# Gate and up of both SwiGLUs by Strassen's scheme for 18 of 22 column tiles, in a one-core fp32r layer kernel

## The chip, the cores and the metric

The kernel runs on one core of one Trainium2 chip. The metric is the device time of one execution in microseconds. The kernel before took 1068.85 us (median of three runs, 1068.67 to 1070.68). A core has TensorE (PE: matmuls, and the weight loads PEld), VectorE (DVE), ScalarE (ACT), GpSimd (POOL) and SyncE (SP). Each of them takes its own list of instructions in order; a semaphore lets an instruction wait for one of another engine.

## The reference

One layer on x of 512 rows by 1024 columns, in float32: a SwiGLU, a token mixer and a second SwiGLU, each between norms, with shift, scale and gate from a conditioning vector c.

```
mod = silu(c) @ w_ada + b_ada                    # 9 x 1024: shift, scale, gate of 3 sub-layers
h = modulate(x, norm_pre_g, shift, scale)        # rms norm, * (1 + scale) + shift
h = swiglu(h, w_gate, w_up, w_down)              # (silu(h @ w_gate) * (h @ w_up)) @ w_down
x = x + 0.5 * (1 + gate) * rms_norm(h, norm_post_g)
x = x + (1 + gate) * rms_norm(hybrid_mixer(...)) # spatial gating and forgetting attention
x = x + 0.5 * (1 + gate) * rms_norm(swiglu(...)) # the second SwiGLU, with its own weights
```

w_gate and w_up are 1024 by 2816 for each SwiGLU, w_down is 2816 by 1024. 2816 columns are 22 column tiles of 128; 1024 rows are 8 blocks (k) of 128.

## The kernel before, in words

x lies transposed, as 8 blocks of 128 features by 512 tokens; "half" below is 256 tokens. Every matmul multiplies fp32r operands that are split into a high part and a low part, and `mm3` makes three matmuls of one product: high by high, high by low, low by high (weights are the stationary side). So a weight comes by DMA on SP's queue as float32 (`raw`, two buffers of 1 MB, `load_next`), ScalarE copies it to its rounded high part (`Pair.hi`, line 192), and VectorE subtracts that from the raw weight for the low part (`Pair.lo`, line 196). `load_next` for the next buffer is issued when both low parts of one are done.

A SwiGLU (`ffn`) goes through its 22 column tiles in three groups of 7, 7 and 8 (`GROUPS`). For a column tile, `gate_up` makes 24 matmuls of 128x512 for gate (PSUM tile `pg`) and 24 for up (`pu`). `activate` then reads them: silu on ScalarE (line 452), times up on VectorE (453), copy to the high part on ScalarE (454), subtraction for the low part on VectorE (457); the tile `h` that results is an operand of down. When a group's tiles are through, down goes over 8 output tiles (`pd`, three matmuls per column tile of the group), which are copied to `y` by ScalarE for the first group (520) and added to it by VectorE for the others (522). The last group's down goes by halves, with the sums of squares for the norm that follows. `ahead` prepares the weights of a later unit after each tile. `between` loads a 512 KB slice of w_ada (`mraw`) and reduces it on VectorE (275); it lies in the first SwiGLU and in the beginning of the mixer only.

The order of the instructions on every engine is the order in which the program is written (`manual_schedule`). In the first SwiGLU the string `START` sets the first three column tiles, beside the norm of x. The second SwiGLU begins beside the mixer's last norm, with four tiles by halves. PSUM has six buffers of 512 columns for all of this (`ps_mm`), and the split weights have eight buffers (`wp`).

## Time and profile before

| | before |
|---|---|
| median of three runs | 1068.85 us |
| the profiled execution, its own time | 1069.54 us |
| its span | 1067.8 us |
| mean granted TensorE clock | 0.965 |
| matmuls | 5246, busy 1012.6 us (95%) |
| VectorE | 983 instructions, busy 567.0 us (53%) |
| ScalarE | 655 instructions, busy 376.4 us (35%) |
| GpSimd | 114 instructions, busy 142.0 us (13%) |
| moved by DMA | 128.82 MB, mean 121 GB/s |

The span is the time from the first to the last instruction of the profiled execution; 1.7 us of its time lie around the span. Busy shares are means over stages with different limits, so a stage is read by its own windows. The first SwiGLU lies from about 60 us to 330 us, the second from about 670 us to the end. A matmul's bar is longer than its step: matmuls are pipelined, so the step from one start to the next is what it costs.

### The profile page before, as it was taken

How to read it: one execution, taken by the hardware profiler on the slowest of the kernel's cores; microseconds unless marked ns; L12 is line 12 of the kernel's file. 1: busy time of each engine (PE TensorE's matmuls, PEld its weight loads, DVE VectorE, ACT ScalarE, POOL GpSimd, SP SyncE). 2: the span in 40 equal slices, each digit the busy share in tenths (PEclk: the TensorE clock that was granted, in tenths of full speed). 3: DMA queues.
4: the chain of work that ended last, by engine and by line, in shares of the span. 5: the costliest groups of instructions: out<-in, count | busy, mean ns of one | idle time of the engine just before them, and what ended most of it. 6: DMA issues, size and time to landing. Idle time of an engine off the chain costs nothing.

```text
span 1067.8 us, 13094 instructions
## 1 busy us (share of the span) xinstructions
PE 1012.6 (95%) x5246; PEld 852.4 (80%) x5246; DVE 567.0 (53%) x983; ACT 376.4 (35%) x655; POOL 142.0 (13%) x114
## 2 busy tenths in 40 slices
PE   6999999999999998899999997799999999999995
PEld 5778888888888997787778687798888888888894
DVE  3876454646443469757756668855222324333434
ACT  5243232322232333444546453534233222222331
POOL 0000000000000036216115135500000000000023
PEclk8899999999999998999999788989999999999998
DMA  8735555456444313241112112114232223232101
GB/s 331 286 139 204 208 202 208 173 179 223 160 142 153 137 62 122 99 147 66 64 35 95 40 41 79 40 41 148 109 119 79 94 84 118 79 109 89 40 21 60
DMA packets 27037, 128.82 MB, mean 121 GB/s; under 512 B 3040, under 2 KB 5472, under 8 KB 18656
## 3 DMA queue, kind: packets, MB, share of 16 engines
q1 hardware_dynamic: 26976, 127.99, 33.6%
q8 instruction: 41, 0.67, 0.2%
q14 instruction: 20, 0.16, 0.0%
HBM read 125.88 MB, written 2.10 MB: 120 GB/s over the span
## 4 chain that ended last, share of the span: by engine, by line
PE 77%; DVE 14%; ACT 3%; DMA 2%; issue 2%; POOL 2%; SPq 0%; DVEq 0%; POOLq 0%; ACTq 0%
PE pu L211 7%; PE pg L209 7%; PE pu L210 7%; PE pg L211 7%; PE pg L210 7%; PE pu L209 7%; PE pd L211 6%; PE pd L209 6%; PE pd L210 6%; DVE mraw L275 2%; DMA mraw<-w_ada 1%; DVE z L362 1%; DVE xm L393 1%; PE pqk L209 1%; PE ps_s L924 1%
## 5 line engine op out<-in xcount | busy, mean ns | idle before, releaser
L192 ACT CAST wu<-raw 128x1024 fp32r<-128x1024 f32 (+2 forms) x164 | 162.3, 1025 | 57.5 <-PE pd L211 53.3
L196 DVE TENSOR_TENSOR wu<-raw,wu 128x1024 fp32r<-128x1024 f32 (+1 forms) x130 | 151.5, 1205 | 58.6 <-ACT wu L192 58.0
L211 PE MATMUL pd<-h,wu 128*128 128x256 f32 (+1 forms) x480 | 160.2, 334 | 0.0
L209 PE MATMUL pd<-h,wu 128*128 128x256 f32 (+1 forms) x480 | 160.1, 333 | 0.0
L210 PE MATMUL pd<-h,wu 128*128 128x256 f32 (+1 forms) x480 | 159.7, 333 | 0.0
L453 DVE TENSOR_TENSOR sg<-sg,pu 128x512 f32<-128x512 f32 (+1 forms) x48 | 30.8, 642 | 230.9 <-PE pu L211 224.2
L250 POOL TENSOR_TENSOR ssum<-ssum,sq 128x256 f32<-128x256 f32 x59 | 47.3, 803 | 776.1 <-ACT sq L249 774.7
L209 PE MATMUL pg<-xm,wu 128*128 128x512 f32 (+1 forms) x360 | 136.1, 378 | 0.0
L211 PE MATMUL pu<-xm,wu 128*128 128x512 f32 (+1 forms) x360 | 136.0, 378 | 0.0
L211 PE MATMUL pg<-xm,wu 128*128 128x512 f32 (+1 forms) x360 | 135.5, 376 | 0.0
L210 PE MATMUL pg<-xm,wu 128*128 128x512 f32 (+1 forms) x360 | 135.1, 375 | 0.0
L210 PE MATMUL pu<-xm,wu 128*128 128x512 f32 (+1 forms) x360 | 134.7, 374 | 0.0
L209 PE MATMUL pu<-xm,wu 128*128 128x512 f32 (+1 forms) x360 | 134.5, 374 | 0.0
L454 ACT CAST h<-sg 128x512 fp32r<-128x512 f32 (+1 forms) x48 | 28.2, 587 | 224.6 <-DVE sg L453 224.6
L210 PEld LDWEIGHTS pd<-h,wu 128*128 128x128 f32 x480 | 90.3, 188 | 10.3
L211 PEld LDWEIGHTS pd<-h,wu 128*128 128x128 f32 x480 | 90.5, 189 | 9.8
L209 PEld LDWEIGHTS pd<-h,wu 128*128 128x128 f32 x480 | 90.1, 188 | 9.7
L196 POOL TENSOR_TENSOR wu<-raw,wu 128x1024 fp32r<-128x1024 f32 (+1 forms) x28 | 69.4, 2488 | 77.3 <-ACT wu L192 77.3
L210 PEld LDWEIGHTS pu<-xm,wu 128*128 128x128 f32 x360 | 68.5, 190 | 13.8
L210 PEld LDWEIGHTS pg<-xm,wu 128*128 128x128 f32 x360 | 68.7, 191 | 13.3
L211 PEld LDWEIGHTS pg<-xm,wu 128*128 128x128 f32 x360 | 68.4, 190 | 13.2
L209 PEld LDWEIGHTS pg<-xm,wu 128*128 128x128 f32 x360 | 68.6, 190 | 12.9
(229 smaller groups left out, 1616.1 us busy)
## 6 DMA issues: line engine op xcount, KB each, us to landing
raw<-wgu SPq DMA_DIRECT2D x43, 1024.0 KB, 4.8
mraw<-w_ada SPq DMA_DIRECT2D x49, 512.0 KB, 3.9
raw<-wd SPq DMA_DIRECT2D x16, 896.0 KB, 4.5
mrawh<-w_ada SPq DMA_DIRECT2D x19, 512.0 KB, 5.1
raw<-wd SPq DMA_DIRECT2D x8, 1024.0 KB, 4.8
raw<-wz SPq DMA_DIRECT2D x4, 1024.0 KB, 4.7
raw<-wqk SPq DMA_DIRECT2D x4, 1024.0 KB, 5.4
raw<-wo SPq DMA_DIRECT2D x4, 1024.0 KB, 4.9
```

Of the source, the lines that this page charges most:

```text
L192: nc.scalar.copy(self.u[j][:, 0, : self.n], self.raw[:, j * self.n : (j + 1) * self.n])
L196: (eng or nc.vector).tensor_sub(u[:, 1, :n], self.raw[:, j * n : (j + 1) * n], u[:, 0, :n].bitcast(F32))
L209: nc.tensor.matmul(ps, lhsT=lh, rhs=rh, start=start, stop=False)
L210: nc.tensor.matmul(ps, lhsT=lh, rhs=rl, start=False, stop=False)
L211: nc.tensor.matmul(ps, lhsT=ll, rhs=rh, start=False, stop=stop)
L250: eng.tensor_add(self.acc, self.acc, sq)
L275: nc.vector.scalar_tensor_tensor(raw, raw, 1.0, crow, op0=ALU.mult, op1=ALU.mult, accum_out=msum[:, j * KT + kt : j * KT + kt + 1])
L362: nc.vector.scalar_tensor_tensor(z[k], ysl(k, cs), G2[i][:, k : k + 1], r, op0=ALU.mult, op1=ALU.mult)
L393: nc.vector.scalar_tensor_tensor(xm[k - 2][:, 1, cs], t[k - 2], shift(i, k - 2), xm[k - 2][:, 0, cs].bitcast(F32), op0=ALU.add, op1=ALU.su ...
L453: nc.vector.tensor_mul(sg, sg, pu[:, :n])
L454: nc.scalar.copy(h[f][:, 0, cs], sg)
L924: nc.tensor.matmul(ps[:, :n], lhsT=sel[:, h : h + 1].broadcast_to([P, P]), rhs=cum[:, :n], start=False, stop=False)
```

## The change

`GROUPS` becomes 4, 4, 4, 4 and 6 column tiles. The four tiles of group 0 are made as before. The other 18 are made in nine pairs. For a pair, the two column tiles, the two halves of the tokens and the two halves of the 1024 features (four blocks k each) make 2x2 blocks: a11, a12, a21, a22 of x (first index: half of the tokens, second: half of the features), and b(kh, fh) of the weights (half of the features, tile). Instead of eight products of blocks there are seven, of sums of blocks. Gate and up lie side by side in one PSUM bank, so a `product` is 2 (gate, up) x 4 blocks k x 3 = 24 matmuls of 256 columns. The order is 1, 2 of the first pair, then per pair 6, 5, 7, 1 of the next pair, 3, 2 of the next pair, 4.

`sums_of_x` makes the four sums S1 to S4 of x's blocks once in each SwiGLU, each in high and low part, in the course of group 0. `prepare` makes the weights of a pair: W1, W2, W3 are split from the raw weights; T5 = b01 - b00 and T7 = b11 - b01 are made by a negating copy on ScalarE (line 687) and a DMA of GpSimd's queue that adds the other block onto it in SBUF (688); T6 and T4 are differences on VectorE (694); all four are then split (702, 703). `evictions` adds up the products: ScalarE copies bank a three times (m1, u2, u3, line 623), VectorE adds bank b or c to the copies (636), and silu, multiplication, copy and subtraction follow for each quarter (637, 613, 615, 616). The list `blocks` holds the matmuls, and `at(b, ...)` puts a piece of work of the other engines ahead of block b. The w_ada slices become halves of 256 KB, of which `between` reduces one after nearly every product of the first SwiGLU. `hp` has 4 buffers of twice the size.

```diff
-GROUPS = (range(0, 7), range(7, 14), range(14, 22))
+GROUPS = (range(0, 4), range(4, 8), range(8, 12), range(12, 16), range(16, 22))
+    def sums_of_x():
+        S = {n: htile([P, KT // 2, 2, HT], F32R, f"S{n}") for n in (1, 2, 3, 4)}
...
+            def split(n, v):
+                hi, lo = (S[n][:, 2 * q : 2 * q + 2, part] for part in range(2))
+                nc.scalar.copy(hi, v)
+                sub(lo, v, hi.bitcast(F32))
...
+            for n, op, b, c in ((1, add, a21, a22), (3, sub, a11, a21)):
+                v[n], low = temp(), temp()
+                op(v[n], b[0], c[0])
+                op(low, b[1], c[1])
+                yield 1.2
+                add(v[n], v[n], low)
+                split(n, v[n])
...
+        def product(p, n):
+            b, fresh = {1: ("a", True), 2: ("b", True), 5: ("c", True), 6: ("a", False), 7: ("a", False), 3: ("c", False), 4: ("a", False)}[n]
+            def work():
+                if fresh:
+                    bank[p, b] = ps_mm.tile([P, 2, HT], F32, tag="mm", name=f"bank_{b}")
+                ps, w = bank[p, b], W[p, n]
+                for e in range(2):
+                    for k in range(KT // 2):
+                        c = slice(k * P, (k + 1) * P)
+                        t = mm3(ps[:, e], w[:, e, 0, c], w[:, e, 1, c], moving(n, k, 0), moving(n, k, 1), fresh and e + k == 0, e == 1 and k == KT // 2 - 1, not fresh)
+                    tick(4 * t)
+                if i == 0 and (n != 6 or p % 4 == 0):
+                    between()
...
+            for name, src, b, fh, cs, after in (("c11", "m1", "b", 0, T1ST, c[2]), ("c22", "u3", "c", 1, T2ND, c[7]),
+                                                ("c12", "u2", "c", 1, T1ST, c[3])):
+                first, second = both(name, src, b, fh, cs)
+                at(after + 1, first)
+                at(after + 2, second)
+            first, second = gated(p, "c21", 0, T2ND, None)
+            at(c[4] + 1, first)
+            at(c[4] + 1, second)
...
+            def added(n, then, minus, plus):
+                def work():
+                    t = sum_of(n, True, then)()
+                    nc.scalar.activation(t, b(*minus), AF.Copy, scale=-1.0)
+                    nc.gpsimd.dma_start(t, b(*plus), accum_op=ALU.add)
...
+            at(c[6] - 5, added(5, 6, (0, 0), (0, 1)))
+            at(c[1] - 2, plain(1, 0, 0))
+            at(c[6] - 4, added(7, 4, (0, 1), (1, 1)))
+            at(c[2] - 2, plain(2, 1, 0))
+            at(c[6] - 3, minus(6, 1, 5))
+            at(c[6] - 2, split(6))
+            at(c[6] - 2, minus(4, 0, 6))
+            at(c[6] - 1, plain(3, 1, 1))
+            at(c[5] - 1, split(5))
+            at(c[7] - 1, split(7))
+            at(c[4] - 5, split(4))
```

In the orders below a row has the line, the operation, the tile written and the tiles read; the numbers behind the names tell the buffers apart, and `128x2x512` is the weight of a product, gate and up side by side. First VectorE, before, in the middle of the first SwiGLU's first group: for a column tile two low parts of weights (196), then the multiplication and the low part of `h` (453, 457).

```order
L196 TENSOR_TENSOR wu_511<-raw_491,wu_511 128x1024
L196 TENSOR_TENSOR wu_514<-raw_491,wu_514 128x1024
L453 TENSOR_TENSOR sg_520<-sg_520,pu_281 128x512
L457 TENSOR_TENSOR h1_519<-sg_520,h1_519 128x512
L196 TENSOR_TENSOR wu_525<-raw_499,wu_525 128x1024
L196 TENSOR_TENSOR wu_528<-raw_499,wu_528 128x1024
L453 TENSOR_TENSOR sg_534<-sg_534,pu_359 128x512
```

Now VectorE with the change, in the second SwiGLU's group 1, from the addition for c22 of the first pair to the last of what stands ahead of W5's low part for the second pair (the weights and T tiles are of the second pair, the `q` tiles of the first but for q_7604, which is c11 of the second).

```order
L636 TENSOR_TENSOR q_7564<-q_7564,bank_c_7512 128x512
L680 TENSOR_TENSOR W2_7573<-raw_7441,W2_7573 128x2x512
L613 TENSOR_TENSOR q_7564<-q_7564 128x256
L616 TENSOR_TENSOR h2_7500<-q_7564,h2_7500 128x256
L694 TENSOR_TENSOR T5_7537<-raw_7441,T5_7537 128x1024
L636 TENSOR_TENSOR q_7497<-q_7497,bank_c_7512 128x512
L703 TENSOR_TENSOR W6_7633<-T5_7537,W6_7633 128x2x512
L694 TENSOR_TENSOR T7_7568<-raw_7441,T5_7537 128x1024
L613 TENSOR_TENSOR q_7497<-q_7497 128x256
L616 TENSOR_TENSOR h2_7500<-q_7497,h2_7500 128x256
L636 TENSOR_TENSOR q_7604<-q_7604,bank_b_7637 128x512
L680 TENSOR_TENSOR W3_7667<-raw_7441,W3_7667 128x2x512
```

Behind these come a low part of a down weight, the multiplications and low parts of c21 and c11, and then W5's low part. Additions, multiplications and low parts of the pair that ends now stand between the low parts and the differences of the pair that comes. ScalarE at the same place, from the copy m1 of the second pair to the high part of its W5:

```order
L623 COPY q_7604<-bank_a_7576 128x512
L637 ACTIVATE q_7497<-q_7497 128x256
L702 CAST W6_7633<-T5_7537 128x2x512
L615 CAST h2_7500<-q_7497 128x256
L637 ACTIVATE q_7604<-q_7604 128x256
L679 CAST W3_7667<-raw_7441 128x2x512
L194 CAST wu_7696<-raw_7571 128x512
L608 ACTIVATE q_7699<-bank_a_7411 128x256
L615 CAST h2_7500<-q_7699 128x256
L615 CAST h3_7705<-q_7604 128x256
L702 CAST W5_7708<-T5_7537 128x2x512
```

The high parts of W6, W3 and W5 now each stand behind a silu or a copy whose input VectorE has to make first.

The third place is VectorE in the first SwiGLU's group 0, with the change, where the last plain tile (sg_609) is activated.

```order
L198 TENSOR_TENSOR wu_521<-raw_492,wu_521 128x512
L444 TENSOR_TENSOR sx_542<-xm0_193,xm4_342 128x512
L445 TENSOR_TENSOR sx_543<-xm0_193,xm4_342 128x512
L447 TENSOR_TENSOR sx_542<-sx_542,sx_543 128x512
L438 TENSOR_TENSOR S1_538<-sx_542,S1_538 128x2x256
...
L438 TENSOR_TENSOR S1_538<-sx_602,S1_538 128x2x256
L507 TENSOR_TENSOR sg_609<-sg_609,pu_525 128x512
L509 TENSOR_TENSOR h1_507<-sg_609,h1_507 128x512
```

Eighteen rows of the sums of x, five of them subtractions behind a copy of ScalarE, now stand ahead of that tile's multiplication.

More of the change, by code (lines that the diff above doesn't have):

```diff
@@ new lines, in ffn, with moving @@
+        raw, W, bank = {}, {}, {}
+        def moving(n, k, part):
+            if n in (1, 2, 4):
+                return xm[k + (n != 1) * KT // 2][:, part, T2ND if n == 4 else T1ST]
+            return forms[{5: 1, 6: 2, 7: 3, 3: 4}[n]][:, k, part, :]
+        def product(p, n):
[10 more added lines that the diff above has]
+                if i == 0 and (n != 6 or p % 4 == 0):
+                    between()
+                W.pop((p, n))
+            return block(24 * HT * MM, work)
@@ new lines, in ffn, with expect_ffn @@
+        for b, (us, work) in enumerate(blocks):
+            for what in todo.pop(b, ()):
+                what()
+            if not forms and b >= KT:
+                finish_side(side_s)
+            work()
+        for b in sorted(todo):
+            for what in todo[b]:
+                what()
+        forms.clear()
+    def expect_ffn(s):
+        for g, fs in enumerate(GROUPS):
+            if g == 0:
+                for f in fs:
+                    expect(a["wgu"][s, f], 2 * D)
+            else:
+                for p in range((fs[0] - PLAIN) // 2, (fs[-1] + 1 - PLAIN) // 2):
+                    for kh in range(2):
+                        expect(a["wst"][s, p, kh], 4 * T)
+            for m in range(KT // 2):
+                expect(a[f"wd{g}"][s, m], 2 * len(fs) * P)
```

458 lines of the change are left out of this document (307 added, 151 removed).

## The prediction

> **What bounds the kernel now.** I read the chain of waits first, then the engines' busy time by stage in three FFN windows (columns: window, length, busy time of PE, PEld, VectorE, ScalarE, GpSimd, granted clock, DMA share, GB/s).
>
> ```profile
> PE 1012.6 (95%) x5246; PEld 852.4 (80%) x5246; DVE 567.0 (53%) x983; ACT 376.4 (35%) x655; POOL 142.0 (13%) x114
> PE 77%; DVE 14%; ACT 3%; DMA 2%; issue 2%; POOL 2%; SPq 0%; DVEq 0%; POOLq 0%; ACTq 0%
> 125.00:190.00 65.00, 65.00 (x283) 52.72 (x282) 34.13 (x48) 19.98 (x26) 0.00 (x0) 1.00 0.55 198
> 750.00:800.00 50.00, 50.00 (x217) 40.57 (x216) 14.03 (x14) 15.00 (x20) 0.00 (x0) 1.00 0.29 100
> 800.00:850.00 50.00, 50.00 (x217) 40.49 (x216) 15.82 (x17) 14.73 (x19) 0.00 (x0) 1.00 0.24 85
> ```
>
> In the FFNs TensorE is busy in the whole window at full clock; VectorE works 34.1 of 65 us in the first FFN (which has the w_ada reductions) and 14 to 16 of 50 in the second. So matmuls taken out count in full, as long as the other engines keep up in the order in which they are now asked to. What a matmul costs is the step between starts:
>
> ```profile
> 339.76 0.40 PE L209 MATMUL pg<-xm,wu 128*128 128x512 f32 x1
> 349.94 0.40 PE L211 MATMUL pg<-xm,wu 128*128 128x512 f32 x1
> ...
> 1014.79 0.27 PE L209 MATMUL pd<-h,wu 128*128 128x256 f32 x1
> 1016.87 0.27 PE L209 MATMUL pd<-h,wu 128*128 128x256 f32 x1
> ```
>
> The first two are 44 steps apart: 10.18 / 44 = 0.231 us for 512 columns. The others are 18 apart: 0.1156 for 256. A step is 0.45 ns per column, and 256 columns lose nothing to the weight load.
>
> **The matmuls removed.** A pair took 2 x 48 x 0.2304 = 22.12 us; seven products of 24 x 0.1152 = 2.765 take 19.35. Eighteen pairs (nine per FFN) save 18 x 2.765 = **49.8 us**. Down's columns stay: the other grouping moves no work of TensorE's. The added matmuls are all of shapes that these rows price, so this term has no range.
>
> **The steady pair.** What was 2 low parts of weights and 2 operations of an activation per tile becomes a tight weave. The prices:
>
> ```profile
> L192 ACT CAST wu<-raw 128x1024 fp32r<-128x1024 f32 x128 | 129.7, 1046 | 57.5 <-PE pd L211 53.3 <-issue 3.6 <-DMA raw<-wgu 0.4
> L520 ACT COPY y<-pd 128x512 f32<-128x512 f32 x16 | 9.4, 588 | 52.1 <-PE pd L211 52.1
> L522 DVE TENSOR_TENSOR y<-y,pd 128x512 f32<-128x512 f32 x16 | 11.0, 688 | 36.6 <-PE pd L211 36.6
> 803.91 2.36 DVE L196 TENSOR_TENSOR wu<-raw,wu 128x1024 fp32r<-128x1024 f32 x2 [7.38 <-ACT wu L192]
> 704.80 0.36 ACT L452 ACTIVATE sg<-pg 128x256 f32<-128x256 f32 x1
> 705.20 0.42 DVE L453 TENSOR_TENSOR sg<-sg,pu 128x256 f32<-128x256 f32 x1 [0.45 <-ACT sg L452]
> 705.66 0.41 ACT L454 CAST h<-sg 128x256 fp32r<-128x256 f32 x1 [0.49 <-DVE sg L453]
> 706.10 0.43 DVE L457 TENSOR_TENSOR h<-sg,h 128x256 fp32r<-128x256 f32 x1 [0.47 <-ACT h L454]
> ```
>
> A 1024-wide copy on ScalarE is 1.05 (the negating copy I price alike), a 1024-wide subtraction or difference on VectorE 2.36 / 2 = 1.18, a 512-wide copy out of PSUM 0.59, a 512-wide addition 0.69; a quarter's silu 0.36, multiplication 0.42, copy 0.41, low part 0.43, with 0.04 from one engine's end to the other's start. Now I walk down the two orders from the end of product 7 of one pair to W5's low part for the next (primes: of the next pair). Both queues are in order, and nearly each row waits for the other engine's last one.
>
> - u3 copy 0.59, c22 addition 0.69, silu 0.36, T7' negation 1.05, W2' high 1.05, low 1.18, c22 multiplication, copy, low part 1.26: 6.18.
> - T6' difference 1.18, c12 addition 0.69, silu 0.36, W6' high 1.05, low 1.18: 4.46.
> - T4' difference 1.18, c12's three 1.26, c11' addition 0.69, silu 0.36, W3' high 1.05, low 1.18: 5.72.
> - c21's three 1.26, c11' multiplication and copy 0.83, W5' high 1.05, low 1.18: 4.32.
>
> Together 20.7, and 16 hand-overs of 0.04 make it 21.3. TensorE has five products in that time (1', 3, 2', 4, 6'), and the first two matmuls of product 5', which need no low part: 5 x 2.765 + 0.23 = 14.05. So it stands still for about **7.3 us** ahead of product 5' in each pair that has a pair before it in its group. Groups of 2, 2, 2 and 3 pairs have 1 + 1 + 1 + 2 = 5 such pairs: 5 x 7.3 = 36.5 us in the second FFN. The bounds: if no row waited for the other engine, VectorE's own rows of the stretch are 5 x 1.18 (W2', T6', W6', T4', W3') + 1.18 (W5') + 3 x 0.69 + 3 x 0.85 + 0.42 = 12.1 us, which fits, and nothing is lost; if the negation and each of VectorE's 1024-wide rows took the 1.22 of the reduction below, it is 21.3 + 0.4 and a stall of 7.7. I take the walk, since an order of single handed-over rows leaves nothing to overlap.
>
> In the first FFN `between` puts one more reduction ahead of each block.
>
> ```profile
> 374.82 1.22 DVE L275 SCALAR_TENSOR_TENSOR mraw<-mraw,crow 128x1024 f32<-128x1024 f32 x1 [2.89 <-DMA mraw<-w_ada]
> ```
>
> At half the width that is 1.22 - (1.18 - 0.69) = 0.73. Five lie on the walk, 3.65 less what falls into waits: I take 3.5, so 10.8 us, times 5 = **54 us** (0 to 5 x 11.0).
>
> **First pairs and group ends.** The first pair of a group has no earlier pair's quarters between its weights, but W5 and W7 still stand behind c11's chain: product 2 to W5's low part is addition 0.69, silu 0.36, high 1.05, low 1.18 plus hops, 3.4, against product 6's 2.77 and 0.23: 0.4 to 0.6, and product 7 another 0.4. I take 0.95, with a reduction or two in the first FFN 1.45: 4 x 0.95 + 4 x 1.45 = 9.6 (0 to 16). At a group's end c21 (0.36 + 1.26 + hops, 1.8) is covered by one part of down, 12 matmuls of 0.1152 = 1.38: 0.4 in each of six, 2.4.
>
> **Group 0.** The START's last rows on VectorE, and a copy:
>
> ```profile
> 67.92 0.68 DVE L453 TENSOR_TENSOR sg<-sg,pu 128x512 f32<-128x512 f32 x1
> 68.64 0.62 ACT L454 CAST h<-sg 128x512 fp32r<-128x512 f32 x1 [1.58 <-DVE sg L453]
> 69.29 0.69 DVE L457 TENSOR_TENSOR h<-sg,h 128x512 fp32r<-128x512 f32 x1 [0.69 <-ACT h L454]
> ...
> 69.54 0.39 PE L209 MATMUL pg<-xm,wu 128*128 128x512 f32 x1
> ```
>
> TensorE begins the fourth plain tile at 69.54, is through 11.06 later at 80.6, and after the 9 matmuls of down on the first three tiles (2.07) needs the fourth at 82.7. VectorE ends the first tile at 69.98; two more activations take 2.1 each (74.2), three half-size low parts 2.1 (76.3), 18 rows of sums at 0.69 take 12.4 (88.7), five of which wait 0.7 for a copy (92.2), multiplication and copy 1.3: 93.5, which is **10.8 us** late. In the second FFN the same rows stand ahead of the last split tile's activations; I take 10.8 again, 21.6 for both (0, if the rows find slack, to 28 rows x 0.69 x 2 = 38.6).
>
> **What a standstill costs after it.** The granted clock (window, length, busy TensorE, clock, DMA share, GB/s) around three gaps that the kernel already has:
>
> ```profile
> 658.00:660.00 2.00, 0.00 (x0) 0.62 0.00 0
> 660.00:662.00 2.00, 0.58 (x3) 0.50 0.00 0
> 662.00:664.00 2.00, 2.00 (x11) 0.50 1.00 291
> 664.00:666.00 2.00, 2.00 (x13) 0.67 0.56 234
> 666.00:668.00 2.00, 2.00 (x19) 1.00 0.00 0
> ...
> 678.00:680.00 2.00, 1.07 (x3) 0.74 0.57 139
> 680.00:682.00 2.00, 2.00 (x11) 0.50 0.92 385
> ...
> 696.00:698.00 2.00, 1.85 (x8) 0.51 0.58 106
> 698.00:700.00 2.00, 2.00 (x12) 0.50 0.98 414
> 700.00:702.00 2.00, 2.00 (x11) 0.50 0.04 12
> 702.00:704.00 2.00, 2.00 (x16) 0.78 0.00 0
> ```
>
> The busy time lost (busy x (1 - clock)) is 0.29 + 1.0 + 0.66 = 1.95, 0.28 + 1.0 = 1.28 and 0.91 + 1.0 + 1.0 + 0.44 = 3.35: mean 2.2. Twelve long gaps (10 pairs, 2 groups 0) cost 12 x 2.2 = **26.4 us** (0 if a gap of 7 us in a period of 26 is too short to be punished, 40 at 3.35). [...]
>
> **The added DMAs.** T5 has some 7 us from the end of its negation to T6's difference, which needs it. No accumulating DMA is in the trace; loads are:
>
> ```profile
> raw<-wgu SPq DMA_DIRECT2D x43, 1024.0 KB, 4.8
> raw<-wsT SPq DMA_DIRECT2D x1, 512.0 KB, 3.2
> raw<-wqk SPq DMA_DIRECT2D x4, 1024.0 KB, 5.4
> ```
>
> It reads two 512 KB operands and writes one: between the 3.2 of 512 KB and, at three times 512 KB, 3.2 + 2 x 1.6 = 6.4. Either is hidden, so I take 0. At 10 us T6 and all that stands behind it would come 3 us later in each pair: 18 x 3 = 54 us. [...]
>
> **Sum**: -49.8 + 36.5 + 54 + 9.6 + 2.4 + 21.6 + 26.4 = +100.7. Against the profiled execution's 1069.5 that is 1170.2; the median lies 0.7 below, so **1169.5 us**.
>
> **Rivals.** *The queues keep up.* VectorE's and ScalarE's busy time fits the pair (12.1 us of 14), and if most hand-overs overlapped, what is left is group 0 and the group ends: -49.8 + 9.6 + 2.4, or 1031 us. For it speaks that VectorE works 14 to 16 us of 50 now; against it that a queue in order stands still while it waits, and the walk has one open row at a time. 12%. *Lighter stalls.* The walk is right in kind, but a third of its waits falls into others: two thirds of the 124 us of the stalls above (36.5 + 54 + 9.6 + 2.4 + 21.6) are 83, and the clock costs 12 x 1.28 to 12 x 2.2: -49.8 + 83 + 15 to 26 is +48 to +59 on 1068.85, 1117 to 1128, with some play 1105 to 1140. For it speaks that in the trace a second copy of ScalarE regularly runs beside VectorE's first row; against it that here the rows belong to one another. 18%. *The accumulating DMA is late*, being the place where T6 waits: from 7 us on it decides; at 10 us half of the 54 us comes on top of stalls that partly take it in, 1200 to 1225. For it speaks that nothing of its kind is in the trace, against it the 6.4 us above. 13%. *The change leaves the time as it was*, savings and stalls cancelling out: 3%; nothing picks that point.
>
> **How the numbers follow.** Forecast 54%, 1169.5, its own range 1140 to 1200 by the bounds of clock and group 0. 1105 to 1212 holds the lighter stalls too and half of the late DMA: 54 + 18 + 6.5 = 78.5%. Faster by over 0.2% (2 us, what a measurement of this kernel can tell): 12%; within: 3%; slower: 85%.
>
> **What would show it.** In the changed profile, TensorE's idle time ahead of line 211 for `bank_c` (product 5) should be 7 to 11 us, 10 times, ended by VectorE's line 703 or ScalarE's 702 of W5; the idle ahead of down in group 0 about 10, ended by lines 508 and 509 of `h`; PEclk about 0.5 in the windows behind. Steps inside products stay at 0.115. Line 694 (T6) should not be ended by a DMA. I am wrong if the gaps ahead of product 5 are under 3 us, or if T6's row waits for GpSimd's queue.

## The result and the profile after

The changed kernel takes **1213.71 us** (median of four runs, 1213.61 to 1216.19), the kernel before in the same comparison 1068.76 (1068.46 to 1070.68): 1.1358 times as long, with a 95% interval of 1.1338 to 1.1377. The forecast was 1169.5 us, with a range up to 1212. The direction and the mechanism of the largest term were right. The forecast is 44 us too low, and the measured time lies 1.7 us above the range.

The page of the changed kernel (busy time by engine, the chain of waits, the two dearest groups of product 5, and the accumulating DMA with its median time to landing):

```profile
span 1211.8 us, 16389 instructions
PE 1030.9 (85%) x6398; PEld 916.5 (76%) x6398; DVE 776.7 (64%) x1438; ACT 517.1 (43%) x917; POOL 181.2 (15%) x148
PE 45%; DVE 27%; ACT 12%; DMA 9%; issue 5%; POOL 2%; SPq 0%; ACTq 0%; DVEq 0%; POOLq 0%
L211 PE MATMUL bank_c<-S,W 128*128 128x256 f32 x288 | 96.8, 336 | 81.3 <-ACT W L702 81.2
L213 PE MATMUL bank_c<-S,W 128*128 128x256 f32 x288 | 95.5, 331 | 8.7 <-DVE W L703 8.7
T<-raw POOLq DMA_DIRECT2D x36, 512.0 KB, 6.1
```

TensorE's share of the chain falls from 77% to 45%, and VectorE's, ScalarE's and the DMA's grow to 27, 12 and 9%. 81.2 of the idle microseconds stand ahead of one group of matmuls, the first of a product 5. The stages (columns as in the prediction's windows), first of the changed kernel, then of the one before. The first stage ends where the statistics of the first half of the first FFN's output begin, at 383 us in the kernel before (its gate and up go on until 358, later than the 330 us named ahead of the prediction):

```profile
69.50:473.20 403.70, 334.02 (x2113) 304.03 (x2112) 267.45 (x479) 161.65 (x253) 26.11 (x24) 0.89 0.54 162
473.20:754.40 281.20, 251.66 (x1440) 210.90 (x1439) 191.72 (x443) 134.12 (x309) 103.40 (x70) 0.92 0.20 69
754.40:1211.80 457.40, 386.66 (x2590) 354.81 (x2590) 274.56 (x442) 194.58 (x322) 51.46 (x51) 0.93 0.37 103
```

```profile
69.50:383.00 313.50, 313.02 (x1453) 258.34 (x1451) 161.21 (x229) 90.49 (x120) 4.45 (x6) 1.00 0.51 184
383.00:661.40 278.40, 255.43 (x1492) 215.10 (x1492) 199.82 (x438) 134.56 (x309) 103.25 (x70) 0.93 0.21 74
661.40:1067.80 406.40, 384.98 (x2038) 330.88 (x2038) 162.83 (x242) 124.19 (x192) 34.11 (x35) 0.97 0.24 83
```

The first FFN grows by 90.2 us, the mixer by 2.8, the second FFN by 51.0. TensorE's idle time in the first FFN goes from 0.5 us to 69.7, and VectorE works 267 us there instead of 161.

**A steady pair** in the second FFN, TensorE at the hand-over from product 6' to product 5', and the granted clock around it (engine columns as above, clock third from the end):

```profile
888.50 0.28 PE L213 MATMUL bank_a<-S,W 128*128 128x256 f32 x1
894.32 0.58 PE L211 MATMUL bank_c<-S,W 128*128 128x256 f32 x1 [5.54 <-ACT W L702]
894.70 0.42 PE L212 MATMUL bank_c<-S,W 128*128 128x256 f32 x1
895.58 0.58 PE L213 MATMUL bank_c<-S,W 128*128 128x256 f32 x1 [0.46 <-DVE W L703]
```

```profile
892.00:894.00 2.00, 0.00 (x0) 0.00 (x0) 1.19 (x3) 1.12 (x3) 0.00 (x0) 0.50 0.63 231
894.00:896.00 2.00, 1.22 (x4) 0.92 (x5) 1.50 (x2) 2.00 (x4) 0.00 (x0) 0.50 0.00 0
896.00:898.00 2.00, 2.00 (x11) 2.00 (x11) 2.00 (x2) 0.65 (x1) 0.00 (x0) 0.50 0.03 8
898.00:900.00 2.00, 2.00 (x18) 2.00 (x18) 0.78 (x2) 0.62 (x1) 0.00 (x0) 0.93 0.00 0
```

The product behind product 7 of the pair before started at 874.34, and the first matmul that needs W5's low part starts 21.2 us later; the walk in the prediction came to 21.3. The clock is at half until about 898, and product 5 of the steady pairs takes 5.2 to 5.9 us instead of 2.86, the wait for its low part included. Ahead of product 5 the ten steady pairs wait 8.35, 7.53, 7.53, 7.13, 6.94 us in the first FFN and 5.54, 5.49, 5.54, 4.83, 4.89 in the second.

**A first pair**, group 2 of the first FFN. Rows of ScalarE, GpSimd, VectorE and TensorE, put in order of time: the negation for T5, its DMA, T6 (which needs T5), the high part of W6, product 5.

```profile
189.51 1.06 ACT L687 ACTIVATE T<-raw 128x1024 f32<-128x1024 f32 x1 [5.23 <-DMA raw<-wst]
190.87 1.19 POOL L688 DMA_DIRECT2D T<-raw  x1 [50.25 <-DVE mraw L272]
198.91 1.23 DVE L694 TENSOR_TENSOR T<-raw,T 128x1024 f32<-128x1024 f32 x1 [1.41 <-DMA T<-raw]
200.25 1.05 ACT L702 CAST W<-T 128x1024 fp32r<-128x1024 f32 x1 [4.13 <-DVE T L694]
209.01 0.58 PE L211 MATMUL bank_c<-S,W 128*128 128x256 f32 x1 [3.52 <-ACT W L702]
```

The raw half arrives 5.2 us after ScalarE is ready for it, because its buffer was held by down's weights until then: the load was issued at 183.91, when the last low part from that buffer ended (183.89). The DMA takes 8.0 us from issue to T6. VectorE waits 1.4 us for it, and ScalarE 4.1 us for VectorE. The rows behind W6 are late with it, and product 5 waits 3.5 us and then runs at half rate, 6.1 us instead of 2.86.

Outside the pairs, the waits of TensorE (in total, times, longest) that the forecast placed in group 0, and two at the end of the first FFN that it did not have:

```profile
PE pd L211 <- ACT h L508: 14.8, 3, 7.9
...
PE pvf L211 <- ACT xm L389: 6.1, 1, 6.1
...
PE ps_stat L329 <- POOL ssum L252: 4.5, 1, 4.5
```

The account, from the starts of TensorE's matmuls (a product counts from its start to that of the next one), with the prediction's clock term put where it arose, 2.2 us for each gap (the two numbers behind the first pairs are the first and the second FFN; "down in parts" is what is left of the sum):

| term (us) | forecast | measured |
|---|---|---|
| matmuls removed | -49.8 | -37.8 |
| steady pairs, with the clock | 112.5 | 94.3 |
| first pairs | 9.6 | 42.0 (31.5 and 10.5) |
| group 0 of both FFNs, with the clock | 26.0 | 24.0 |
| down in parts and the last groups | 2.4 | about 13 |
| end of the first FFN, start of the mixer | 0 | 8.3 |
| sum | 100.7 | 144.0 (1211.8 - 1067.8) |

The theory from here: two queues in order pass single rows to and fro (steady pairs), and in first pairs the raw weights come late and the accumulating DMA is long, one behind the other. Rivals: the w_ada reductions fill VectorE; the row order of the sums in group 0 is an even larger part; the half rate and not the waits; narrow matmuls are dear by themselves.

### The profile page after: what moved, and what is told of

Its sections match the earlier page's. It is cut to its first block, busy times and chain, and to the rows that moved or that the text cites. A ratio compares the mean times of both kernels' runs of the same rounds, so it can differ in the third digit from the quotient of the medians.

```text
span 1211.8 us, 16389 instructions
## 1 busy us (share of the span) xinstructions
PE 1030.9 (85%) x6398; PEld 916.5 (76%) x6398; DVE 776.7 (64%) x1438; ACT 517.1 (43%) x917; POOL 181.2 (15%) x148
## 4 chain that ended last, share of the span: by engine, by line
PE 45%; DVE 27%; ACT 12%; DMA 9%; issue 5%; POOL 2%; SPq 0%; ACTq 0%; DVEq 0%; POOLq 0%
DMA mraw<-w_ada 5%; PE pd L211 4%; PE pd L212 4%; PE pd L213 4%; DMA T<-raw 3%; PE bank_c L213 3%; DVE W L703 3%; DVE mraw L272 3%; PE bank_c L211 3%; PE bank_c L212 2%; ACT W L702 2%; PE bank_a L213 2%; PE bank_a L211 2%; PE bank_a L212 2%; DVE T L694 2%
## 5 line engine op out<-in xcount | busy, mean ns | idle before, releaser
L211 PE MATMUL pd<-h,wu 128*128 128x512 f32 (+1 forms) x448 | 160.4, 358 | 17.5 <-ACT h L508 14.8
L211 PE MATMUL bank_c<-S,W 128*128 128x256 f32 x288 | 96.8, 336 | 81.3 <-ACT W L702 81.2
L213 PE MATMUL pd<-h,wu 128*128 128x512 f32 (+1 forms) x448 | 158.6, 354 | 2.5 <-DVE wu L198 2.5
L212 PE MATMUL pd<-h,wu 128*128 128x512 f32 (+1 forms) x448 | 158.6, 354 | 0.0
L211 PEld LDWEIGHTS bank_c<-S,W 128*128 128x128 f32 x288 | 67.8, 235 | 87.1 <-ACT W L702 84.5
L194 ACT CAST wu<-raw 128x512 fp32r<-128x512 f32 (+3 forms) x124 | 95.5, 794 | 46.2 <-DMA raw<-wd 17.1
L703 DVE TENSOR_TENSOR W<-T,W 128x1024 fp32r<-128x1024 f32 x72 | 86.8, 1223 | 42.6 <-ACT W L702 42.6
L272 DVE SCALAR_TENSOR_TENSOR mraw<-mraw,crow 128x512 f32<-128x512 f32 (+1 forms) x124 | 90.8, 739 | 25.3 <-DMA mraw<-w_ada 25.0
L198 DVE TENSOR_TENSOR wu<-raw,wu 128x512 fp32r<-128x512 f32 (+3 forms) x92 | 73.2, 805 | 46.8 <-ACT wu L194 45.7
L213 PE MATMUL bank_c<-S,W 128*128 128x256 f32 x288 | 95.5, 331 | 8.7 <-DVE W L703 8.7
L212 PE MATMUL bank_c<-S,W 128*128 128x256 f32 x288 | 93.1, 323 | 0.0
L702 ACT CAST W<-T 128x1024 fp32r<-128x1024 f32 x72 | 73.3, 1040 | 31.1 <-DVE T L694 30.9
L213 PE MATMUL bank_a<-S,W 128*128 128x256 f32 x288 | 82.7, 287 | 2.6 <-DVE W L703 2.4
L211 PE MATMUL bank_a<-S,W 128*128 128x256 f32 x288 | 81.7, 284 | 0.5 <-ACT q L623 0.5
L212 PE MATMUL bank_a<-S,W 128*128 128x256 f32 x288 | 81.4, 283 | 0.0
L211 PE MATMUL bank_a<-xm,W 128*128 128x256 f32 x288 | 81.3, 282 | 0.0
L213 PE MATMUL bank_a<-xm,W 128*128 128x256 f32 x288 | 81.3, 282 | 0.0
```

The costliest lines, as they stand in the source:

```text
L194: nc.scalar.copy(self.u[j][:, 0, : self.n], self.raw[:, j * self.n : (j + 1) * self.n])
L198: (eng or nc.vector).tensor_sub(u[:, 1, :n], self.raw[:, j * n : (j + 1) * n], u[:, 0, :n].bitcast(F32))
L211: nc.tensor.matmul(ps, lhsT=lh, rhs=rh, start=start, stop=False, skip_group_check=onto)
L212: nc.tensor.matmul(ps, lhsT=lh, rhs=rl, start=False, stop=False, skip_group_check=onto)
L213: nc.tensor.matmul(ps, lhsT=ll, rhs=rh, start=False, stop=stop, skip_group_check=onto)
L272: nc.vector.scalar_tensor_tensor(raw, raw, 1.0, c, op0=ALU.mult, op1=ALU.mult, accum_out=to[:, j * KT + kt : j * KT + kt + 1])
```

## The experiments

**Another order of the same rows.** The same instructions, in another order: a table says for each row by which product it counts, how many blocks from its start, and where in the block. High parts of weights come earlier, low parts no longer directly behind them, the quarters' rows later. The places at which loads and the accumulating DMAs are issued move with the rows.

```diff
+PREP = {..., "W5h": (5, -2, 0.391), "W5l": (5, -2, 0.957), "W7h": (7, -3, 0.662), "W7l": (7, -1, 0.026), ...}
...
+EVICT = {..., "c11a": (2, 2, 0.419), "c11s": (2, 3, 0.907), "c11m": (2, 5, 0.506), "c11c": (2, 6, 0.105), "c11l": (2, 6, 0.763), ...}
...
-                at(after + 1, first)
-                at(after + 2, second)
...
-            at(c[5] - 1, split(5))
-            at(c[7] - 1, split(7))
```

> The changed kernel with the same instructions on the same engines in the pairs (only the dummy order of rows changes): the quarters' additions, multiplications and low parts stand one to four blocks later in ScalarE's and VectorE's queues, the weights' high parts one to two blocks earlier, and a low part no longer directly behind its high part. Buffers and transfers are the same. Theory (single handed-over rows in queues that are in order): TensorE's waits ahead of product 5 (some 5.5 us in the second FFN, 7.5 in the first, ten of them) fall below 1 us, those of the first pairs below 2, and with them the half-rate stretches: 68 us of steady waits, 19 of clock and some 25 of the 42 of first pairs go, so 1095 to 1115 us from 1213.7. Rival 1 (VectorE has too much to do for a pair): no order helps, 1200 or more. Rival 2 (the accumulating DMA lands too late): the waits move to the differences T6 and T4 and fall by less than half, 1160 to 1190.

Measured: 1106.69 us (1104.46 to 1109.85), 1.0371 times the kernel before (1.0328 to 1.0415), and 107 us under the changed kernel. TensorE's waits (in total, times, longest), and 56 us of the second FFN, the last group's pairs in the main:

```profile
PE pd L215 <- ACT h L512: 13.3, 3, 7.9
PE bank_a L215 <- ACT q L614: 6.0, 6, 1.5
PE bank_a L217 <- DVE W L677: 5.5, 4, 2.0
```

```profile
984.00:1040.00 56.00, 56.00 (x450) 54.96 (x449) 41.12 (x50) 33.51 (x49) 6.01 (x5) 1.00 0.65 160
```

The wait for W5 is gone, and TensorE is busy in the whole of that stretch at full clock, with VectorE at 41 of 56 us. In the first FFN one steady pair has a wait left, of 1.7 us ahead of product 3. So the stalls of the steady pairs came from the order of the rows and not from the amount of work. What is left over the kernel before is in group 0 (the wait for `h`) and the first pairs (the waits on `bank_a` in the first FFN), at down's parts and at the end of the first FFN.

**Keeping the clock up in the gap.** Dummy matmuls of 256 columns run ahead of product 5 in all but the first pairs.

```diff
+                if n == 5 and p not in (0, 2, 4, 6):
+                    idle = psax("idle")
+                    for _ in range(56 if i == 0 else 40):
+                        nc.tensor.matmul(idle[:, :HT], lhsT=xm[0][:, 0, :P], rhs=xm[0][:, 0, T1ST], start=True, stop=True)
```

> The changed kernel with matmuls into an unused PSUM tile ahead of product 5 of each pair that is not the first of its group: 56 of 256 columns in the first FFN (6.5 us), 40 in the second (4.6 us), inside the standstill and a little shorter than it. They compute nothing that is used. Theory (a standstill of 5 us or more costs half rate behind it): product 5 takes 3.6 us instead of 5.2 to 5.6, ten times, so 15 to 20 us less: 1194 to 1199. Rival (product 5 is slow for its low part, whose wait is 0.7 us, and for a cause that is not the clock): within 5 us of 1213.7.

Measured: 1204.89 us (1201.16 to 1208.45), 8.8 under the changed kernel, about half of what was expected, and outside the ranges of both the theory and the rival. Product 5 of the steady pairs has two waits left, one ahead of it and one of 0.76 us for the low part behind its second matmul. In four pairs the first is 0.4 us or less, and product 5 takes 3.97 to 4.00 us: 2.86, the 0.76 and some slower steps. In six it is 0.71 to 1.64 us, and in five of these product 5 goes to half rate and takes 5.3 to 5.5. One of the five, just behind the dummy matmuls (TensorE's rows), then the clock in two stretches there and in two around the sixth pair, which kept it (waits of 0.83 us, ended at 241.55, and of 0.76, ended at 242.81):

```profile
888.81 0.39 PE L211 MATMUL bank_c<-S,W 128*128 128x256 f32 x1 [0.74 <-ACT W L706]
890.07 0.39 PE L213 MATMUL bank_c<-S,W 128*128 128x256 f32 x1 [0.76 <-DVE W L707]
```

```profile
887.66:891.08 3.42, 1.92 (x14) 1.51 (x13) 2.52 (x3) 3.42 (x5) 0.00 (x0) 1.00 0.08 32
891.08:894.49 3.41, 3.41 (x18) 3.41 (x17) 2.19 (x3) 0.67 (x2) 0.00 (x0) 0.50 0.00 0
...
239.13:242.54 3.41, 2.09 (x16) 1.68 (x14) 2.20 (x4) 2.53 (x5) 0.00 (x0) 1.00 0.49 192
242.54:245.96 3.42, 3.15 (x26) 3.15 (x27) 3.19 (x5) 1.95 (x3) 0.00 (x0) 1.00 0.00 0
```

In the first place two waits of 0.74 and 0.76 us within two microseconds were followed by half rate from 891.08 on, 1.0 us after the second. The stretches are not chosen freely: the changes of the granted clock lie whole multiples of 3.413 us apart, in this run (88.94 and 891.08 are 235 of them apart), in the traces of the changed kernel (half rate from 891.44 to 898.27, two of them) and of the one before, and in those of the later sums of x and of the run without slices below. In the first place both waits lie in one such stretch, with 1.92 us of work in it; in the sixth pair such a point, 242.54, falls into the second wait. Another pair, at 322.27, has waits as long as the sixth (0.84 and 0.76 us), both in the 3.41 us ahead of 324.46, with 1.8 us of work, and went to half rate there. These two pairs have waits of the same length, and differ in how the waits fall on these points. Which amount of work keeps the clock is not shown: in the run without the accumulating DMA below, waits of 2.58 and 0.76 us (ended at 284.55 and 285.81) were followed by steps of 0.12 us, at full rate. So the half rate is a part of the price, and this way gets it back in half of the pairs only, since the weight is still late.

**The sums of x later.** The 28 rows of sums follow the last plain tile's activation instead of preceding it.

```diff
-            side_s = beside(sums_of_x())
             prologue()
             for f in rest:
                 activate(f, gate_up([f], ALL)[f], ALL)
                 units.pop(f)
+            side_s = beside(sums_of_x())
...
```

> The changed kernel with the sums of x begun behind the last plain tile's activation instead of ahead of it, in both FFNs. Theory (the sums' rows in VectorE's queue hold back that activation): the gaps ahead of down in group 0 (7.9 us in the first FFN, 3.1 and 6.7 in the second) and about 2.4 us of half rate behind each go, if the sums then fit beside group 0's down: 1193 to 1200. Rival (the activation is late for ScalarE's copies and the weights' low parts there): less than 5 us.

Measured: 1208.23 us (1204.68 to 1209.33), 5.5 under the changed kernel instead of 13 to 21. The wait for `h` goes, and another comes, at the first product of the first pair:

```profile
109.33 0.58 PE L211 MATMUL bank_a<-xm,W 128*128 128x256 f32 x1 [4.87 <-ACT W L679]
```

It is there in the second FFN too (4.86 us). The sums now stand ahead of W1's rows. The wait is not that of one row: in the 22.6 us of down ahead of it, from 81.90 on, VectorE is busy for 19.5.

**Narrow matmuls by themselves.** The kernel before, with gate and up in halves of 256 columns.

```diff
+            parts = cs if cs is HALVES else (cs,)
...
+                    for part in parts:
+                        for k in ks:
...
-                    activate(f, gate_up([f], ALL)[f], ALL, more if f < fs[-1] else None)
+                    activate(f, gate_up([f], HALVES)[f], ALL, more if f < fs[-1] else None)
```

> The kernel before, with gate and up of the 37 column tiles that are made over all tokens computed as two halves of 256 columns into the same PSUM tile: twice the matmuls and weight loads, the same columns and nothing else. It prices the step of 256 columns: 3552 of them. At 0.1156 us, the step of 256 in the trace of before: 37 x 96 x (0.1156 - 0.1152) = +1.4 us, 1070. At 0.1192, the step inside the products of the changed kernel: +14 us, 1083. If it is 1070, the products' slower step comes from what else runs at that time or from their operands, and not from the width.

Measured: 1070.3 us (1069.45 to 1072.63), 1.0020 times the kernel before (1.0005 to 1.0035). Rows of gate and of up of one column tile, 18 and 20 steps apart:

```profile
744.52 0.27 PE L209 MATMUL pg<-xm,wu 128*128 128x256 f32 x1
746.60 0.27 PE L209 MATMUL pg<-xm,wu 128*128 128x256 f32 x1
...
749.88 0.28 PE L210 MATMUL pu<-xm,wu 128*128 128x256 f32 x1
752.24 0.28 PE L209 MATMUL pu<-xm,wu 128*128 128x256 f32 x1
```

The steps are 2.08 / 18 = 0.1156 and 2.36 / 20 = 0.118 us. Both occur for gate and for up, one of them throughout most tiles, and their mean over the run is 0.1174. The time is 1.0 us longer, where 0.1192 in each of them would have made it 14. A product of the changed kernel that waits for nothing, its first matmul and its last, 23 steps on:

```profile
136.22 0.28 PE L211 MATMUL bank_a<-xm,W 128*128 128x256 f32 x1
138.94 0.28 PE L213 MATMUL bank_a<-xm,W 128*128 128x256 f32 x1
```

That is 0.1183 a step; the products take 2.84 to 2.88 us for 24, 0.1192 in the mean. Their step is nearer the longer of the two, and its cause was not found.

**No w_ada slices beside the products.** The blocks of the first FFN's products neither load nor reduce a slice.

```diff
                 if i == 0 and (n != 6 or p % 4 == 0):
-                    between()
+                    without()
```

> The changed kernel without the w_ada slices in the products of the first SwiGLU: 57 of the 112 halves are neither loaded nor reduced (shift, scale and gate of later sub-layers come out wrong for it). Theory (a reduction ahead of each block, and its wait for a slice that lands late, hold up VectorE's queue): the steady waits of the first FFN fall from 7.5 us to the second FFN's 5.5, five times, and the first pairs' 3.5 to 4.4 to 2 or less, four times, with some half-rate time: 20 to 30 us less, 1184 to 1194. Rival (first pairs wait for the accumulating DMA or for the weights' loads, and the slices only add their 0.77): the first pairs keep their 3.5 to 4.4 us, 1198 to 1206.

Measured: 1200.99 us in one run (so without an interval), 12.7 under the changed kernel. It leaves out 57 of the 112 halves of w_ada. The waits of the steady pairs in the first FFN fall to 6.2, 5.5, 5.5, 4.9 and 4.9 us, which are those of the second FFN. Those of the first pairs are 5.13, 4.76, 4.96 and 3.18, no smaller than 3.61, 3.52, 4.42 and 4.14 before. So the slices explain the difference between the FFNs in the steady pairs, and nothing of the first pairs' waits ahead of product 5.

**No accumulating DMA.** T5 and T7 are made by one subtraction on VectorE.

```diff
-                    nc.scalar.activation(t, b(*minus), AF.Copy, scale=-1.0)
-                    nc.gpsimd.dma_start(t, b(*plus), accum_op=ALU.add)
+                    nc.vector.tensor_sub(t, b(*plus), b(*minus))
```

> The changed kernel with T5 and T7 made by one subtraction of VectorE each, in place of ScalarE's negation and GpSimd's accumulating DMA. Theory (the walk): of the walk's rows T7's 1.05 on ScalarE is replaced by 1.15 on VectorE, which now come in one queue with c22's, so the steady waits stay within 1 us of 5.5 and 7.5, the first pairs of the first FFN, whose T6 waited up to 1.4 us for the DMA, get 1 to 2 us shorter each: 1205 to 1217. Rival (the accumulating DMA is what the pair waits for): the steady waits fall by 3 us or more, 1150 to 1180.

Measured: 1197.95 us in one run (without an interval too), 15.7 under the changed kernel and more than was expected. The edit takes ScalarE's negation out with the DMA, so the gain is that of both. The waits ahead of product 5 in the first FFN's first pairs fall to 2.31, 2.61, 2.57 and 2.35 us, in the steady pairs by about 1 us in the second FFN. VectorE gets 36 rows more by this, and still gains. What ScalarE waits for most now, among DMAs:

```profile
ACT W L679 <- DMA raw<-wst: 47.6, 11, 6.4
```

That is the late raw half, which the DMA was behind. It is taken apart below.

**Both in the better order.** The new order of rows, with the subtraction in place of the negation and the DMA.

```diff
 # on the kernel with the other order
-                    nc.scalar.activation(t, b(*minus), AF.Copy, scale=-1.0)
-                    nc.gpsimd.dma_start(t, b(*plus), accum_op=ALU.add)
+                    nc.vector.tensor_sub(t, b(*plus), b(*minus))
```

> The reordered kernel of the first experiment with T5 and T7 made by one subtraction of VectorE each, in place of ScalarE's negation and GpSimd's accumulating DMA. Theory A (in the first pair of a group the chain from the weights' load over the negation and a DMA of 8.0 us to T6 sets the end): the waits ahead of product 6 in the first FFN (2.7, 2.4, 2.1 and 3.1 us in the reordered kernel) and the half rate behind them fall by more than half, 10 to 20 us less than 1106.7: 1087 to 1097. Theory B (VectorE is close to its limit in the first FFN, 2.4 us more per pair fill it): new waits in the steady pairs, 1105 to 1125.

Measured: 1112.69 us (1111.69 to 1114.9), 1.0414 times the kernel before (1.0396 to 1.0431), 6 us over the new order alone. Product 6 of the first FFN's first pairs, from its start to that of product 5, falls from 6.7, 6.0, 3.9 and 6.9 us to 3.04 to 3.09. Ahead of it three of the four still wait 1.5 to 1.9 us. How much of the fall is the DMA's is not shown: in the new order alone the differences wait for the DMA three times, 2.2 us in all over both FFNs, and in group 1 the low part of W6 stands behind a slice of w_ada that comes 2.0 us late. But a new wait comes, at product 3 of each of these first pairs (first row); the second row has 60 us there, in which VectorE is busy for 48.7:

```profile
137.57 0.58 PE L215 MATMUL bank_c<-S,W 128*128 128x256 f32 x1 [3.34 <-DVE q L623]
```

```profile
250.00:310.00 60.00, 53.18 (x380) 49.98 (x378) 48.66 (x84) 23.52 (x36) 0.00 (x0) 0.97 0.46 157
```

The time is in theory B's range. That VectorE is full is not shown by this: in the same 60 us of the new order alone it is busy for 50.8, with TensorE at 57.6. The two further 1.2 us rows of a pair and an order that was not made for them come together here, and no run separates them.

**Two further orders.** The first has an own table for each FFN, sums of x late with 8 of the 28 rows on GpSimd, a slice of w_ada after every product, and one sum of squares on VectorE instead of GpSimd. The second keeps the tables, has all sums of x on VectorE and that sum of squares on GpSimd again, moves two low parts of the mixer's weights to VectorE, and loads down's weights of a group of four tiles in two loads of 1 MB instead of four.

```diff
...
+            eng = nc.gpsimd if q else nc.vector
-            for n, op, b, c in ((1, add, a21, a22), (3, sub, a11, a21)):
+            for n, op, b, c in ((1, eng.tensor_add, a21, a22), (3, eng.tensor_sub, a11, a21)):
```

> The reordered kernel of the first experiment, with four more edits: the sums of x begin behind the last plain tile's activation, a third of their rows go to GpSimd (8 of 28), a w_ada half is reduced after every product of the first FFN and only after six of eight parts of down, the sum of squares of the first half of the new x goes to VectorE at the end of the first FFN, and each FFN has its own order of rows. Theory: group 0's gaps (7.9 and 5.3 us) shrink to 5 and 3 with a new wait ahead of product 1 for its weight, the first pairs of the first FFN lose most of their 2 to 3 us, and the 4.9 us ahead of the statistics at its end go: 15 to 30 us less than 1106.7, 1077 to 1092. Rival (the rest sits elsewhere: in the slower step of the products, 0.119 us, and in shorter covers, which none of these edits touch): 1098 or more.

```diff
+            per = 2 if g == last_group else 4
...
-                if m % 2 == 0:
-                    du[g, m // 2] = Pair(nk * P)
+                if m % per == 0:
+                    du[g, m // per] = Pair(nk * P, per)
```

> The second reordered kernel without work for GpSimd: all sums of x on VectorE again, two of the six low parts of the mixer's first weights on VectorE instead of GpSimd, the sums of squares as in the first; and the down weights of groups of four tiles come in two transfers of 1 MB instead of four of 512 KB, so that the buffers turn less often and the next group's first weights are asked for earlier. Theory (VectorE's rows took 1.6 to 1.8 us instead of 0.69 beside GpSimd's in the last run, and the first weights of a group come late): the gaps ahead of product 1 in group 1 (4.4 and 3.1 us) and of product 6 shrink to 2 or less: 1070 to 1088. Rival (the late weights are a matter of the transfer itself, not of when it is asked for): 1092 or more.

Measured: 1098.64 us (1090.37 to 1104.0), 1.0295 times the kernel before (1.0262 to 1.0328), and 1099.66 (1095.66 to 1102.24), 1.0287 (1.0254 to 1.0319). Both are worse than their main theory said, and in the range of its rival. In the first, VectorE's rows beside GpSimd's are slow (VectorE's rows, then a GpSimd row that runs meanwhile):

```profile
98.95 1.76 DVE L280 SCALAR_TENSOR_TENSOR mraw<-mraw,crow 128x512 f32<-128x512 f32 x1
102.33 1.77 DVE L461 TENSOR_TENSOR sx<-sx,xm 128x512 f32<-128x512 f32 x1
104.14 0.69 DVE L462 TENSOR_TENSOR sx<-sx,xm 128x512 f32<-128x512 f32 x1
```

```profile
101.93 1.62 POOL L456 TENSOR_TENSOR sx<-sx 128x512 f32<-128x512 f32 x1
```

Here a 512-wide row takes 1.76 us while GpSimd works, and 0.69 when it begins in the pause of GpSimd from 103.55 to 104.28, so GpSimd's help is paid for by VectorE. In the second it is the weights of first pairs that are late (TensorE's waits):

```profile
PE bank_b L221 <- DVE W L685: 11.0, 7, 2.5
PE bank_a L219 <- ACT W L679: 6.4, 2, 4.9
```

Neither order beats the kernel before; 1098.64 us is the fastest version with the seven products that was run.

**Raw weights early.** The second half of down's weights of groups 0 to 3 isn't loaded; the rows that split them read a tile of x, so buffers for raw weights come free earlier. This also takes 16 loads of 512 KB off the DMA engines. Once with the accumulating DMA, once with the subtraction.

```diff
-        def __init__(self, n):
-            self.n, self.raw, self.u, self.done = n, arrived.pop(0), [None, None], 0
+        def __init__(self, n, raw=None):
+            self.n, self.raw, self.u, self.done = n, arrived.pop(0) if raw is None else raw, [None, None], 0
+            self.loaded = raw is None
...
-            if self.done == 2:
+            if self.done == 2 and self.loaded:
...
-                    du[g, m // 2] = Pair(nk * P)
+                    du[g, m // 2] = Pair(nk * P, None if g == last_group or m < 4 else xm[0].rearrange("p a t -> p (a t)").bitcast(F32))
...
-            for m in range(KT // 2):
+            for m in range(KT // 2 if g == len(GROUPS) - 1 else KT // 4):
                 expect(a[f"wd{g}"][s, m], 2 * len(fs) * P)
```

> What it leaves out: the second half of down's weights (units 4 to 7) of groups 0 to 3 in both FFNs is not loaded; the two rows that split each of them still run, in the same places, but read a tile of x, so down's output is not the reference's. A buffer for raw weights is then free some 8 us earlier at each group's end, and the two raw halves of the next group's first pair are loaded that much sooner. Theory A, the late raw weights start the first pairs' chain late and the rows behind it only pass that on: ScalarE's negation for T5 no longer waits for its raw half (5.2 us in the changed kernel's group 2), the idle ahead of product 5 in the four first pairs of the first FFN falls from 3.5 to 4.4 us to under 1.5 and most of the half rate behind it goes too; the first pairs' 42 us fall by half or more: 1184 to 1196. Rival B, the accumulating DMA and the order of the rows decide, and the late raw half is hidden behind them: the idle stays at 3 us and over, 1206 to 1214.

> Leaves out the same half of down's weights of groups 0 to 3 as the kernel with early raw weights, and makes T5 and T7 by one subtraction on VectorE in place of the negation and the accumulating DMA. Theory A (late raw half and DMA lie one behind the other, and are all of the first pairs' loss): the idle ahead of product 5 in the first FFN's first pairs is under 0.8 us, and the time is that of the subtraction alone (1198) less 12 to 25: 1173 to 1186. Rival B (the raw half is hidden anyway): within 5 us of the subtraction alone, 1193 to 1200, with the idle near the 2.3 to 2.6 us that it left.

Measured: 1197.73 us (1193.03 to 1199.1), 16.0 under the changed kernel, and 1185.53 (1182.61 to 1188.3), 28.2 under it and 12.4 under the subtraction alone. The first is 1.7 us slower than its theory's range, with waits of 1.98 to 2.16 us ahead of product 5 that lie between the marks of both theories; the second is inside. In the first of them, the same place as above (GpSimd's row for T5, VectorE's T6, TensorE's product 5):

```profile
181.17 1.19 POOL L689 DMA_DIRECT2D T<-raw  x1 [43.51 <-DMA raw<-wst]
194.98 1.22 DVE L695 TENSOR_TENSOR T<-raw,T 128x1024 f32<-128x1024 f32 x1
204.15 0.39 PE L212 MATMUL bank_c<-S,W 128*128 128x256 f32 x1 [1.98 <-ACT W L703]
```

The DMA is issued 12.3 us ahead of product 1 (193.46) instead of 5.8 (190.87 to 196.67), and T6, 13.8 us behind the issue, waits for nothing. There are also fewer loads beside the DMA here; the run does not separate this from the earlier start. 2.0 us of the wait are left, because VectorE now works without a pause from 193.23 to 202.71: low parts, differences, two slices and the addition of c11, one row behind the other. With the subtraction in addition the waits are 0.64, 0.94, 1.15 and 0.92 us. The four first pairs of the first FFN, what product 6's slot (with the wait for product 5 in it) and product 5's take over 2.86 us each:

| us over four pairs | slot of product 6 | product 5 | sum |
|---|---|---|---|
| forecast | | | 5.8 |
| changed kernel | 18.2 | 12.1 | 30.3 |
| subtraction, no DMA | 11.4 | 9.7 | 21.1 |
| raw weights early | 8.9 | 10.2 | 19.1 |
| both | 4.3 | 6.0 | 10.3 |

Each alone takes about 10 us away, both together 20. The two lie one behind the other in the chain, and their costs add. With both, more than half of what is left is product 5's own: the wait for the low part, and half rate in one of the four pairs.

## Why the prediction was wrong, step by step

- **First pairs: the step that failed.** The prediction says of them that they have "no earlier pair's quarters between" their weights and takes 9.6 us (0 to 16); they cost 42. It walked from product 2 to W5's low part as if W6 and T4 were on time. They were not: raw halves wait for buffers that down's weights hold (5.2 us in group 2), and the accumulating DMA follows on that. The runs with early raw weights and with the subtraction show both, 10 us each of the 30 that products 6 and 5 lose there in the first FFN, against 5.8 in the forecast. It also put the clock's price on twelve gaps only; product 5 of the first pairs runs at half rate too, and with the wait for its low part loses 12 us in that FFN. The second FFN's first pairs lose 10.5 us, 7.2 of it in group 2, where the low part of W2 stands in VectorE's queue behind two reductions of w_ada that wait 2.5 and 1.4 us for their slices; no run took that out.
- **The added DMA: "either is hidden, so I take 0".** Right in the steady pairs by the profile, where T6 never waits for it, and wrong in the first ones. The prediction bounded it by 3.2 to 6.4 us. Its median is 6.1, its range 4.8 to 10.3, and in the first pairs of groups 1 and 2 it was 8.7 and 8.0. The rival of the late DMA named 1200 to 1225, and the time lies in it, but by its own mechanism it does not hold: T6 waits for the DMA five times, 5.6 us in all, where the rival had 3 us in each of 18 pairs. Taking the DMA and the negation out brought 15.7 us in one run.
- **The matmuls removed.** Priced at 0.1152 us a matmul, "this term has no range". Products take 0.1192: -37.8 instead of -49.8. The rows of down with 256 columns priced another stream of matmuls, and four thousandths of a microsecond decide here, since seven products are set against eight. The halves of gate and up step at 0.1174 in the mean, so the width is at most a part of the reason; the rest stays open.
- **The steady pairs: right in kind.** The walk gave 21.3 us to W5's low part, and the trace has 21.2. The gap came out at 5.5 instead of 7.3 in the second FFN for two reasons: the five products before it are longer (14.3 instead of 13.8), and product 5 starts with the high part and waits for the low part inside itself. With the half rate it is 94 us against 112. That the order and not the work was the reason is shown by the new order, which takes all of the waits ahead of product 5 away. Its 107 us hold some 17 of the first pairs too, by the same count of slots.
- **Slices of w_ada.** They were to add 3.5 us to a walk; without them the steady waits in the first FFN fall by 2 us, to those of the second FFN.
- **Group 0.** 21.6 us and the clock, 26 in all, against 24. The place and the waiting row (`pd` for `h`, 7.9 us in the first FFN) are as named, and the 18 rows of sums ran from 76.0 to 90.7 us where the walk had 76.3 to 92.2. That it is VectorE's load there and not just one row that stands wrong was not said, and the later sums show it: a new wait of 4.9 us.
- **Half rate.** 2.2 us for each gap was near: product 5 of the steady pairs is 2.3 to 3.1 us longer than without a wait. About 0.76 of it is the wait for the low part, as the pairs at full clock of the dummy matmuls' run have it, which leaves 1.5 to 2.3.
- **Group ends and the end of the first FFN: 2.4 against about 21.** Priced by one activation's cover. The last group's first half is shorter now (six tiles, a cover of 16.6 us by its matmuls instead of 22.2), so the waits that end it come to light: 4.5 us for GpSimd's sum of squares and 6.1 for the mixer's first input, against 1.7 and three waits of together 4.6 in the kernel before. The first further order moved that sum to VectorE, and 7.8 us were idle ahead of the same statistics, 4.9 in the new order alone, so the engine of the sum does not explain the wait. No run takes these terms apart; they stay a reading of the timeline, and their cause is open.
- The two marks of a wrong prediction: gaps under 3 us did not come in the ten steady pairs; T6's row did wait for GpSimd's queue, in five first pairs. The 9.6 us in the first rival's sum are those of the first pairs, not of group 0 as its words say.

## What to carry to other kernels

An estimate of a change of order has to walk the start of each group as carefully as its middle: which buffer the first load waits for, what holds it, and what each late step adds behind that. When two engines pass single rows to and fro in order, count the passes between the last matmul of one round and the first of the next; moving the rows by one to four blocks was worth 107 us here, more than any row taken out. A gain of one product in eight is 2.1 us in 22, and is lost with a single wait of the kind that the steady pairs had here: 4.8 to 8.4 us, with 1.5 to 2.3 us of half rate behind it.

## What the runs showed of the hardware that was not expected

- In the first further order VectorE's rows of 512 columns with two operands in SBUF take 1.55 to 1.77 us, from 97.47 to 104.10, while GpSimd runs a row of its own, and the row at 104.14, which begins in GpSimd's pause, takes 0.69. What makes them longer was not shown.
- In the run with the dummy matmuls waits of 0.74 and 0.76 us, ended at 888.81 and 890.07, were followed by half rate at 891.08: five of the six pairs with a first wait of 0.71 to 1.64 us went to half rate, and none of the four with 0.4 or less. Longer waits did not always: with the subtraction alone, waits of 2.58 and 0.76 us, ended at 284.55 and 285.81, left the clock full, with steps of 0.12 us behind them. In the five traces named above the changes of the clock lie whole multiples of 3.413 us apart, and of two pairs with waits of equal length (0.83 or 0.84 us, and 0.76) the one with both waits between two such points lost the clock and the other did not; a limit for the work between two such points does not come out of these runs.
- A matmul of 256 columns steps at 0.1156 or at 0.118 us in the halves of gate and up, in most tiles at one of them throughout, and at 0.1192 in the mean of the products, with the same shapes and with no wait. The cause stays open.
- The accumulating DMA of 512 KB takes 6.1 us in the median of 36 and 4.8 to 10.3 in all. In the same trace the 32 plain loads of that size for down's weights have a median of 3.6 us, and the 12 slices of w_ada of that size one of 7.5; what sets the difference was not shown.
